# Spreading the state-space decay rows over the partitions: selector matmuls or broadcast reads from DRAM

## The chip, the cores and the metric

The kernel runs on one core of one Trainium2 chip. The metric is device time in microseconds (us) of one execution, smaller is better. The engines of the core are TensorE (PE in the profile; its weight loads are shown apart as PEld), VectorE (DVE), ScalarE (ACT), GpSimd (POOL) and SyncE (SP), which here only issues transfers. TensorE's clock has two levels, 1.2 and 2.4 GHz; the profile gives the granted clock as a share of the higher one.

## The reference, cut to what matters

Two layers, each a token-mixing sub-layer and an MLP, on 256 latent tokens and 256 context tokens of width 1024. The second layer doesn't need the context's output. One of the four mixers is a bidirectional state-space scan (SSD) in chunks of 128 tokens with 16 heads in 4 groups:

```
a_cum  = cumsum(dt * a)                       # over the 128 tokens of a chunk
seg    = a_cum[l] - a_cum[s]
decay  = exp(where(lower, seg, -inf))         # 128 x 128 for each chunk and head
y_diag = einsum(cb, decay, xdt)               # cb = C B^T of the group
y_off  = einsum(cm, states_in, exp(a_cum))
```

It runs once forward and once on the reversed sequence, and the two results are added. The other mixers (neighbourhood attention, pooling, Fourier), the gates, the output projection and the MLP are not touched by the change.

## The kernel before, in words

All arithmetic is float32. The large products (input projection, branch projections, MLP) split each 128-wide weight tile into a high part (ScalarE, L151) and a remainder (VectorE, L152) and run three passes on TensorE for each of 8 contraction tiles (`mm3`, L182): 24 matmuls of 512 columns in the first layer, of 512 or 256 in the second. Weight tiles `st` come through SP's queue (L145) into 3 buffers; their split pairs `whi`/`wlo` have 3 buffers too. The order of work is made by hand: `Driver` runs generators (`ssd_unit` for each of the 4 groups, two `attn_unit` after each), which yield so that one unit's projections fill TensorE while another's vector work runs. A planner then places the instructions on each engine's queue by priority; weight loads and splits get a priority 150 instructions earlier.

`dt_unit` computes the cumulative decays once for each layer. It transposes them to 64 rows (32 x direction + head) by 512 tokens in PSUM (`pr`, L486), and writes them as a high and a low part into R, and their exponentials into RE (L488 to L494).

In `ssd_unit`, a half-step `i` handles two heads `j`, each with two directions `d` (L594 to L617). For each (j, d), TensorE multiplies a column of the selector matrix, broadcast to 128 columns, with R: this spreads one row of the decays over all 128 partitions of a PSUM tile (L603). A second matmul adds the triangular mask (L604). ScalarE takes exp with the per-token bias `nAv`, one instruction for each chunk of 128 tokens (L607), into a tile `ex`. A third matmul spreads the row of RE (L610), and VectorE multiplies it with `Ct` into `e0` (L612). GpSimd adds the two directions (L614), VectorE multiplies by `cb` (L615), and after the next yield TensorE uses both products (L628, L631). A layer has 4 groups x 2 half-steps x 2 heads x 2 directions = 32 such (j, d). NT, the number of chunks, is 4 in the first layer and 2 in the second; NX is 512 and 256 tokens. The tiles `ex` and `e0` come from the pool `t2` (2 KB on each partition, 40 buffers), which most other 512-wide temporaries use too.

After the last group, `yt` (L663) is split (L196, L197) and goes into the SSD branch projection.

Of the kernel before, what the change touches and what calls it, by code (L numbers as in the profile page):

```python
# [9 lines left out]
F32 = mybir.dt.float32  # L10
F32R = mybir.dt.float32r
# [4 lines left out]
P = 128  # L16
# [42 lines left out]
def _const_layout():  # L59
    n = 0  # L60
    for name, w in (("ident", 128), ("triu", 128), ("tril", 128), ("cos", 256), ("sin", 256), ("sel2", 2),
                    ("maskf", 128), ("maskb", 128), ("sel", 32)):
        _CONST[name] = (n, w)
        n += w
    return n
# [8 lines left out]
def hybrid_backbone_kernel(ctx: ExitStack, tc: tile.TileContext, I, out, dbg=None):  # L74
# [10 lines left out]
    t2p = ctx.enter_context(tc.tile_pool(name="t2", bufs=40))  # L85
# [4 lines left out]
    drm = ctx.enter_context(tc.tile_pool(name="drm", bufs=1, space=bass.MemoryType.DRAM))  # L90

# [3 lines left out]
    def T2(shape, name, dt=F32):  # L95
        return t2p.tile(shape, dt, tag="t2", name=name)
# [10 lines left out]
    def PS(shape=(P, 512)):  # L107
        return pss.tile(list(shape), F32, tag="sm", name="psx")
# [5 lines left out]
    once = T2([P, NCONST - NKEEP], "once")  # L114
# [259 lines left out]
    def layer(l, need_ctx, h, ws, load_x, final, prepare=None):  # L374
# [51 lines left out]
        def dt_unit(ps):  # L426
# [55 lines left out]
            R = lay.tile([P, 4, P], F32R, tag="R", name="R", bufs=1)  # L482
# [4 lines left out]
            prv = pr[0:64, :].rearrange("p (t c) -> p t c", t=4)  # L487
            act.copy(R[0:64], prv)  # L488
            dve.tensor_tensor(R[64:128], prv, R.bitcast(F32)[0:64], op=ALU.subtract)
            RE = lay.tile([P, 4, P], F32R, tag="RE", name="RE", bufs=1)  # L490
            er = T2([64, 4, P], "er")
            act.activation(er, prv, AF.Exp)
            act.copy(RE[0:64], er)
            dve.tensor_tensor(RE[64:128], er, RE.bitcast(F32)[0:64], op=ALU.subtract)  # L494
            dtc.update(R=R, RE=RE, nA=v4(nA), coef=v4(coef), dec=v4(dec))

# [26 lines left out]
        def ssd_unit(g, ready=None):  # L523
# [16 lines left out]
            coefv, decv, nAv, R, RE = dtc["coef"], dtc["dec"], dtc["nA"], dtc["R"], dtc["RE"]  # L540
# [17 lines left out]
            for d in range(2):  # L558
                xw = T4([P, 4, 256], "xw")
                for t0, n in (((0, 1), (2, 2)) if d == 0 else ((1, 3),)):  # L560
                    dve.tensor_tensor(xw[:, t0:t0 + n].rearrange("p t (h c) -> p t h c", h=4),
                                      xk[:, t0:t0 + n].rearrange("p t (h c) -> p t h c", h=4),
                                      coefv[:, t0:t0 + n, d, 4 * g:4 * g + 4].unsqueeze(3).to_broadcast([P, n, 4, 64]),
                                      op=ALU.mult)
                xws.append(xw)
            yield "w", 1
# [27 lines left out]
            for i in range(2):  # L594
                M, CE = {}, {}
                for j in range(2):
                    hd = 4 * g + 2 * i + j
                    ed = []
                    for d in range(2):
                        c = 16 * d + hd  # L600
                        one = selr[:, c:c + 1].to_broadcast([P, P])
                        pv = PS().rearrange("p (t c) -> p t c", t=4)
                        pe.matmul(pv[:, 0:NT], one, R[:, 0:NT], start=True, stop=False)  # L603
                        pe.matmul(pv[:, 0:NT], identr, maskr[:, d:d + 1].to_broadcast([P, NT, P]), start=False, stop=True)  # L604
                        ex = T2([P, 4, P], "ex")
                        for t in range(NT):
                            act.activation(ex[:, t], pv[:, t], AF.Exp, bias=nAv[:, t, d, hd:hd + 1])  # L607
                        ed.append(ex)
                        pa = PS()
                        pe.matmul(pa.rearrange("p (t c) -> p t c", t=4)[:, 0:NT], one, RE[:, 0:NT], start=True, stop=True)  # L610
                        e0 = T2([P, 512], "e0")
                        dve.tensor_tensor(e0[:, 0:NX], Ct[:, 0:NX], pa[:, 0:NX], op=ALU.mult)  # L612
                        CE[j, d] = e0
                    pool.tensor_tensor(ed[0][:, 0:NT], ed[0][:, 0:NT], ed[1][:, 0:NT], op=ALU.add)  # L614
                    dve.tensor_tensor(ed[0][:, 0:NT], ed[0][:, 0:NT], cb[:, 0:NX].rearrange("p (t c) -> p t c", c=P),  # L615
                                      op=ALU.mult)
                    M[j] = ed[0]  # L617
                yield "w", 1
# [629 lines left out]
    sp.dma_start(once, I["consts"][:, NKEEP:NCONST])  # L1248
    identr = cst.tile([P, P], F32R, name="identr")
    act.copy(identr, ident)  # L1250
    maskr = cst.tile([P, 2, P], F32R, name="maskr")
    act.copy(maskr, once[:, 0:256].rearrange("p (d c) -> p d c", d=2))
    selr = cst.tile([P, 32], F32R, name="selr")
    act.copy(selr, once[:, 256:288])
# [30 lines left out]
def _constants():  # L1285
    c = np.zeros((P, NCONST), np.float32)

    def put(name, a):
        o, w = _CONST[name]
        c[:, o:o + w] = a  # L1290
# [12 lines left out]
    sel = np.zeros((P, 32))  # L1303
    for d in range(2):
        for h in range(16):
            sel[32 * d + h, 16 * d + h] = 1
            sel[64 + 32 * d + h, 16 * d + h] = 1
    put("sel", sel)
# [96 lines left out]
```

## Time and profile before

| | us |
|---|---|
| median of 3 runs | 2168.09 |
| lowest, highest | 2165.13, 2174.14 |
| the profiled execution | 2167.03 |
| its span, first to last instruction | 2164.9 |
| mean granted TensorE clock | 0.989 |

Busy times of an engine are unions over its instructions. A matmul's time runs from its start to its modelled end, and the next one starts before that; so the busy share of PE says that it had something in hand, and the distance from start to start says how fast it works. Where a row names a releaser, the time before it is idle time of that engine, and the releaser is what ended it. SPq rows are instructions of SP's queue; the time from there to landing is given apart.

### The profile page before, as it was taken

To read this page: it belongs to the slowest core of one execution; us is meant where nothing else is said; L and a number is where in the kernel's file an instruction comes from. 1 tells how busy PE (TensorE), PEld (TensorE's weight loads), DVE (VectorE), ACT (ScalarE), POOL (GpSimd) and SP (SyncE) were. 2 spreads that over 40 slices of the span, in tenths; PEclk is the share of its full clock that TensorE was granted. 3 is DMA by queue.
4 is the path that set the end of the run, shared out by engine and by line. 5 is a ranking of instruction groups with operands and counts; after the bars stand their busy time and mean duration, and the time that the engine had idled before them with its cause. 6 is when DMAs were issued, how large, how long until landed. Compare 5 with 4: busy or idle time off the path is not lost. (4 is left out here: it accounts for less than half of the span.)

```text
span 2164.9 us, 31409 instructions
## 1 busy us (share of the span) xinstructions
PE 2106.0 (97%) x12248; PEld 1740.0 (80%) x12248; DVE 1273.1 (59%) x2281; ACT 997.9 (46%) x1756; POOL 238.6 (11%) x244
## 2 busy tenths in 40 slices
PE   6999999999999999999999999999999999998998
PEld 3677777777888888878877887878787899987987
DVE  3686585854336544475333357687768557566557
ACT  3565565654323323334232233566656545445543
POOL 0001000010010010112011121001000000112111
PEclk8999999999999999999999999999999999999999
DMA  7523232332332531334343333423333466566554
GB/s 268 170 78 117 88 127 88 124 105 70 97 94 91 179 106 52 98 117 150 110 149 123 95 115 135 140 79 117 124 100 123 136 184 209 173 208 214 188 190 140
DMA packets 85379, 285.35 MB, mean 132 GB/s; under 512 B 9904, under 2 KB 13680, under 8 KB 85232
## 3 DMA queue, kind: packets, MB, share of 16 engines
q1 hardware_dynamic: 85232, 283.36, 40.9%
q8 instruction: 96, 1.57, 0.3%
q14 instruction: 51, 0.42, 0.1%
HBM read 281.19 MB, written 2.13 MB: 131 GB/s over the span
## 5 line engine op out<-in xcount | busy, mean ns | idle before, releaser
L152 DVE TENSOR_TENSOR wlo<-st,whi 128x1024 fp32r<-128x1024 f32 (+3 forms) x382 | 478.8, 1254 | 482.9 <-ACT whi L151 466.6
L151 ACT CAST whi<-st 128x1024 fp32r<-128x1024 f32 (+3 forms) x382 | 385.8, 1011 | 767.9 <-PE pm L182 539.6
L182 PE MATMUL pm<-h_hi,whi 128*128 128x512 f32 (+1 forms) x1944 | 680.4, 351 | 3.6 <-DVE qb L682 2.1
L182 PE MATMUL pm<-h_lo,whi 128*128 128x512 f32 (+1 forms) x1944 | 676.3, 348 | 3.1 <-DVE h_lo L364 3.0
L182 PE MATMUL pm<-h_hi,wlo 128*128 128x512 f32 (+1 forms) x1944 | 677.2, 349 | 0.3 <-DVE wlo L152 0.3
L182 PEld LDWEIGHTS pm<-h_hi,whi 128*128 128x128 f32 x1944 | 369.4, 190 | 56.5 <-issue 9.3
L182 PEld LDWEIGHTS pm<-h_lo,whi 128*128 128x128 f32 x1944 | 369.9, 190 | 47.2 <-DVE h_lo L364 3.9
L182 PEld LDWEIGHTS pm<-h_hi,wlo 128*128 128x128 f32 x1944 | 369.4, 190 | 47.0 <-issue 1.9
L191 PE MATMUL pm<-whi,part 128*128 128x512 f32 x784 | 243.4, 391 | 0.0
L182 PE MATMUL pm<-part,whi 128*128 128x512 f32 (+1 forms) x896 | 222.8, 338 | 2.9 <-DVE part L197 1.2
L182 PEld LDWEIGHTS pm<-part,whi 128*128 128x128 f32 x896 | 154.4, 190 | 23.1 <-DVE part L197 2.5
L191 PEld LDWEIGHTS pm<-whi,part 128*128 128x128 f32 x784 | 146.3, 188 | 30.6 <-issue 0.4
L191 PE MATMUL pm<-wlo,part 128*128 128x512 f32 x392 | 152.7, 390 | 0.0
L182 PE MATMUL pm<-part,wlo 128*128 128x512 f32 (+1 forms) x448 | 150.7, 336 | 0.5 <-DVE wlo L152 0.5
L1149 POOL TENSOR_TENSOR relu<-relu 128x512 f32<-128x512 f32 (+1 forms) x64 | 87.4, 1366 | 395.9 <-ACT relu L1146 370.8
L819 POOL TENSOR_TENSOR mg<-mg,gth 128x512 f32<-128x512 f32 (+1 forms) x48 | 53.3, 1111 | 533.1 <-DVE gth L818 466.4
L509 DVE SCALAR_TENSOR_TENSOR cacc<-cv,cols,cacc 128x512 f32<-128x512 f32 (+1 forms) x128 | 93.8, 733 | 8.9 <-ACT cacc L507 6.7
L182 PEld LDWEIGHTS pm<-part,wlo 128*128 128x128 f32 x448 | 85.1, 190 | 9.3 <-DVE wlo L152 0.7
L191 PEld LDWEIGHTS pm<-wlo,part 128*128 128x128 f32 x392 | 73.6, 188 | 15.7 <-DVE wlo L152 0.4
L283 PE MATMUL psx<-ad,csil 128*32 128x256 f32 x688 | 57.8, 405 | 9.3 <-DMA ad<-ada_w 8.9
L818 DVE SCALAR_TENSOR_TENSOR gth<-gth,pm 128x512 f32<-128x512 f32 (+1 forms) x48 | 26.6, 554 | 65.6 <-PE pm L182 65.6
L614 POOL TENSOR_TENSOR ex<-ex 128x512 f32<-128x512 f32 (+1 forms) x32 | 33.4, 1045 | 253.2 <-ACT ex L607 178.3
(270 smaller groups left out, 2594.3 us busy)
## 6 DMA issues: line engine op xcount, KB each, us to landing
st<-in_w SPq DMA_DIRECT2D x184, 512.0 KB, 3.6
ad<-ada_w SPq DMA_DIRECT2D x86, 512.0 KB, 3.6
st<-mlp_up_w SPq DMA_DIRECT2D x64, 512.0 KB, 3.5
st<-mlp_down_w SPq DMA_DIRECT2D x64, 512.0 KB, 3.6
bia<-rpb SPq DMA_DIRECT2D x16, 512.0 KB, 4.5
st<-ssd_out_w SPq DMA_DIRECT2D x16, 512.0 KB, 3.6
st<-na_out_w SPq DMA_DIRECT2D x16, 512.0 KB, 3.5
st<-mix_out_w SPq DMA_DIRECT2D x16, 512.0 KB, 3.7
```

Of the source, the lines that this page charges most:

```text
L151: act.copy(hi, st)
L152: dve.tensor_tensor(lo, st, hi.bitcast(F32), op=ALU.subtract)
L182: pe.matmul(ps, w(x, kw), rhs(a[y], ka), start=(i == 0 and j == 0), stop=(i == n - 1 and j == 2))
L191: pe.matmul(ps, a[y][k][:, P * t:P * t + P], w(x, i), start=(k == 0 and j == 0), stop=(k == KD - 1 and j == 2))
L283: pe.matmul(pa[32 * k:32 * k + 32, 0:256], csil[:, 4 * kc + k, :], st(k), start=(kc == 0), stop=(kc == 1), tile_position=(0, 32 * k))
L509: dve.scalar_tensor_tensor(acc, c[:, 0:ns, k:k + 256], col("convw", 5 * m + k), acc, op0=ALU.mult, op1=ALU.add)
L614: pool.tensor_tensor(ed[0][:, 0:NT], ed[0][:, 0:NT], ed[1][:, 0:NT], op=ALU.add)
L818: dve.scalar_tensor_tensor(th, th, 1.0, py[:, 0:NX], op0=ALU.add, op1=ALU.mult)
L819: pool.tensor_tensor(mg[m], mg[m], th, op=ALU.add)
L1149: pool.tensor_tensor(r2, r, r, op=ALU.mult)
```

## The change

The decay rows no longer go through TensorE. `dt_unit` copies the 64 x 512 cumulative decays (VectorE) and their exponentials (ScalarE) into two `t2` tiles and writes both to DRAM (`sums`, 128 KB each, SP's queue). `ssd_unit` reads each needed row back with a broadcast transfer that writes the same row to all 128 partitions: 8 transfers for each half-step (2 heads x 2 directions x {decays, exponentials}), on SP's queue, into `t2` tiles `line`. Those for half-step 0 are traced one yield earlier, those for half-step 1 behind half-step 0's vector work. VectorE adds bias and mask in place, one instruction for each chunk of 128 tokens; ScalarE takes one exp over the whole tile. The product with `Ct` reads the second line from SBUF in place of PSUM. R, RE, `identr`, `maskr` and `selr` go; `maskm` (1 KB on each partition) stays resident; `t2` gets 42 buffers.

```diff
-    t2p = ctx.enter_context(tc.tile_pool(name="t2", bufs=40))
+    t2p = ctx.enter_context(tc.tile_pool(name="t2", bufs=42))
+    sums = [[drm.tile([64, 512], F32, name=f"sums{l}{x}") for x in range(2)] for l in range(DEPTH)]
-    once = T2([P, NCONST - NKEEP], "once")
+    maskm = cst.tile([P, 2, P], F32, name="maskm")
...
-            R = lay.tile([P, 4, P], F32R, tag="R", name="R", bufs=1)
...
-            act.copy(R[0:64], prv)
-            dve.tensor_tensor(R[64:128], prv, R.bitcast(F32)[0:64], op=ALU.subtract)
-            RE = lay.tile([P, 4, P], F32R, tag="RE", name="RE", bufs=1)
-            er = T2([64, 4, P], "er")
-            act.activation(er, prv, AF.Exp)
-            act.copy(RE[0:64], er)
-            dve.tensor_tensor(RE[64:128], er, RE.bitcast(F32)[0:64], op=ALU.subtract)
+            for x in range(2):
+                rt = T2([64, 512], "rt")
+                if x:
+                    act.activation(rt, pr[0:64, :], AF.Exp)
+                else:
+                    dve.tensor_copy(rt, pr[0:64, :])
+                sp.dma_start(sums[l][x], rt)
...
+            def load_lines(i):
+                for j in range(2):
+                    for d in range(2):
+                        r = 32 * d + 4 * g + 2 * i + j
+                        for x in range(2):
+                            lines[j, d, x] = T2([P, 4, P], "line")
+                            sp.dma_start(lines[j, d, x].rearrange("p t c -> p (t c)")[:, 0:NX],
+                                         sums[l][x][r:r + 1, 0:NX].to_broadcast([P, NX]))
...
+            load_lines(0)
             yield "w", 1
...
-                        c = 16 * d + hd
-                        one = selr[:, c:c + 1].to_broadcast([P, P])
-                        pv = PS().rearrange("p (t c) -> p t c", t=4)
-                        pe.matmul(pv[:, 0:NT], one, R[:, 0:NT], start=True, stop=False)
-                        pe.matmul(pv[:, 0:NT], identr, maskr[:, d:d + 1].to_broadcast([P, NT, P]), start=False, stop=True)
-                        ex = T2([P, 4, P], "ex")
+                        ex, e0 = lines.pop((j, d, 0)), lines.pop((j, d, 1)).rearrange("p t c -> p (t c)")
                         for t in range(NT):
-                            act.activation(ex[:, t], pv[:, t], AF.Exp, bias=nAv[:, t, d, hd:hd + 1])
+                            dve.scalar_tensor_tensor(ex[:, t], ex[:, t], nAv[:, t, d, hd:hd + 1], maskm[:, d], op0=ALU.add,
+                                                     op1=ALU.add)
+                        act.activation(ex[:, 0:NT], ex[:, 0:NT], AF.Exp)
                         ed.append(ex)
-                        pa = PS()
-                        pe.matmul(pa.rearrange("p (t c) -> p t c", t=4)[:, 0:NT], one, RE[:, 0:NT], start=True, stop=True)
-                        e0 = T2([P, 512], "e0")
-                        dve.tensor_tensor(e0[:, 0:NX], Ct[:, 0:NX], pa[:, 0:NX], op=ALU.mult)
+                        dve.tensor_tensor(e0[:, 0:NX], Ct[:, 0:NX], e0[:, 0:NX], op=ALU.mult)
                         CE[j, d] = e0
...
+                if i == 0:
+                    load_lines(1)
                 yield "w", 1
```

## Rows read from the trace of the kernel before

**Rows 1.** The page, busy us, share of the span, instructions, by engine
```profile
PE 2106.0 (97%) x12248; PEld 1740.0 (80%) x12248; DVE 1273.1 (59%) x2281; ACT 997.9 (46%) x1756; POOL 238.6 (11%) x244
```
**Rows 2.** SSD stretches: us, PE, PEld, DVE, ACT, POOL busy; clock, DMA, GB/s
```profile
145.00:500.00 355.00, 353.73 (x2134) 276.35 (x2133) 237.56 (x531) 207.68 (x458) 31.53 (x28) 0.99 0.32 101
1440.00:1680.00 240.00, 239.77 (x1582) 195.91 (x1581) 178.66 (x424) 146.92 (x305) 20.51 (x25) 1.00 0.36 114
```
**Rows 3.** PE's waits, 95 to 520 us: us in total, times, longest
```profile
PE pm L182 <- DVE part L197: 0.8, 1, 0.8
```
**Rows 4.** The three selector lines, all of the span: duration min/median/max, first and last start
```profile
L603 PE MATMUL psx<-R,selr x64: 276/390/580, 151.3 to 1669.7; 128*128 128x512 f32 x32, 128*128 128x256 f32 x32
...
L604 PE MATMUL psx<-maskr,identr x64: 276/336/398, 151.5 to 1669.9; 128*128 128x512 f32 x32, 128*128 128x256 f32 x32
...
L610 PE MATMUL psx<-RE,selr x64: 274/388/501, 152.0 to 1670.0; 128*128 128x512 f32 x32, 128*128 128x256 f32 x32
```
**Rows 5.** Timeline, first layer: start us, duration us, engine, line, what
```profile
151.30 0.40 PE L603 MATMUL psx<-R,selr 128*128 128x512 f32 x1
151.30 0.19 PEld L604 LDWEIGHTS psx<-maskr,identr 128*128 128x128 f32 x1
151.53 0.39 PE L604 MATMUL psx<-maskr,identr 128*128 128x512 f32 x1
...
151.76 0.39 PE L182 MATMUL pm<-h_hi,whi 128*128 128x512 f32 x1
...
151.99 2.19 ACT L607 ACTIVATE ex<-psx,nA 128x128 f32<-128x128 f32 x8
...
155.84 0.40 PE L182 MATMUL pm<-h_hi,wlo 128*128 128x512 f32 x1
...
156.49 0.49 PE L610 MATMUL psx<-RE,selr 128*128 128x512 f32 x1 [0.24 <-DVE e L612]
```
**Rows 6.** Timeline, second layer, PE
```profile
1666.66 0.28 PE L604 MATMUL psx<-maskr,identr 128*128 128x256 f32 x1
1666.78 0.28 PE L610 MATMUL psx<-RE,selr 128*128 128x256 f32 x1
```
**Rows 7.** DVE by line and shape, all of the span: count, busy us, mean ns, idle before
```profile
L446 DVE SCALAR_TENSOR_TENSOR e<-e,s 128x128 f32<-128x128 f32 x12 | 3.4, 285 | 0.1
...
L917 DVE SCALAR_TENSOR_TENSOR f<-cs,fu,psx 128x129 f32<-128x129 f32 x18 | 5.7, 344 | 0.0
```
**Rows 8.** DVE by line and shape, 145 to 500 us
```profile
L612 DVE TENSOR_TENSOR e<-Ct,psx 128x512 f32<-128x512 f32 x32 | 21.5, 681 | 0.5
...
L615 DVE TENSOR_TENSOR ex<-ex,cb 128x512 f32<-128x512 f32 x16 | 11.1, 692 | 10.8 <-POOL ex L614 10.6
```
**Rows 9.** ACT by line and shape, all of the span
```profile
L646 ACT ACTIVATE sq<-ys 128x512 f32<-128x512 f32 x8 | 5.1, 632 | 7.0 <-DVE ys L645 7.0
```
**Rows 10.** ACT's waits, 145 to 500 us: us in total, times, longest
```profile
ACT whi L151 <- PE pm L182: 50.1, 17, 8.4
```
**Rows 11.** The page's DMA issues: count, KB each, median us to landing
```profile
gb<-gd SPq DMA_DIRECT2D x12, 256.0 KB, 4.7
...
gd<-grow SPq DMA_DIRECT2D x4, 8.0 KB, 3.2
```
**Rows 12.** SP's queue in time: start us, us, line, what
```profile
70.90 0.91 SPq L673 DMA_DIRECT2D bia<-rpb  x2
...
1936.25 8.93 SPq L268 DMA_DIRECT2D adh<-ada_w  x12
```
**Rows 13.** The stretch behind the 12 transfers of rows 12: columns as in rows 2
```profile
1940.00:1945.00 5.00, 5.00 (x26) 3.87 (x29) 3.50 (x6) 1.05 (x1) 0.00 (x0) 1.00 0.99 362
```
**Rows 14.** First use of the bias tiles, and the first layer's last `yt` and its split
```profile
L713 DVE CUSTOM_DVE_ANT_0 sc<-psx,bia x2: 421/423/425, 106.3 to 107.7; 128x256 f32<-128x256 f32 x2
...
L663 DVE SCALAR_TENSOR_TENSOR yt<-ys,cols,psx x2: 741/744/747, 487.7 to 488.4; 128x512 f32<-128x512 f32 x2
...
L196 ACT CAST part<-yt x8: 616/620/626, 505.2 to 509.8; 128x512 fp32r<-128x512 f32 x8
```

More of the change, by code (lines that the diff above doesn't have):

```diff
@@ L61, in _const_layout @@
     for name, w in (("ident", 128), ("triu", 128), ("tril", 128), ("cos", 256), ("sin", 256), ("sel2", 2),
-                    ("maskf", 128), ("maskb", 128), ("sel", 32)):
+                    ("maskf", 128), ("maskb", 128)):
         _CONST[name] = (n, w)
@@ L486, in dt_unit @@
                 pe.transpose(pr[0:64, P * t:P * t + P], av[:, t, :], ident)
-            prv = pr[0:64, :].rearrange("p (t c) -> p t c", t=4)
-            act.copy(R[0:64], prv)
-            dve.tensor_tensor(R[64:128], prv, R.bitcast(F32)[0:64], op=ALU.subtract)
-            RE = lay.tile([P, 4, P], F32R, tag="RE", name="RE", bufs=1)
-            er = T2([64, 4, P], "er")
-            act.activation(er, prv, AF.Exp)
-            act.copy(RE[0:64], er)
-            dve.tensor_tensor(RE[64:128], er, RE.bitcast(F32)[0:64], op=ALU.subtract)
-            dtc.update(R=R, RE=RE, nA=v4(nA), coef=v4(coef), dec=v4(dec))
+            for x in range(2):
[5 more added lines that the diff above has]
+                sp.dma_start(sums[l][x], rt)
+            dtc.update(nA=v4(nA), coef=v4(coef), dec=v4(dec))
         yt = {}
@@ L539, in ssd_unit @@
             yield "w", LAGS[0] + (LAGS[1] if ready else 0)
-            coefv, decv, nAv, R, RE = dtc["coef"], dtc["dec"], dtc["nA"], dtc["R"], dtc["RE"]
+            coefv, decv, nAv = dtc["coef"], dtc["dec"], dtc["nA"]
+            lines = {}
+            def load_lines(i):
[6 more added lines that the diff above has]
+                                         sums[l][x][r:r + 1, 0:NX].to_broadcast([P, NX]))
             xk = T4([P, 4, 256], "xk")
@@ L1247, in hybrid_backbone_kernel @@
     prepare(0)
[L1248 to L1254, printed above, removed]
+    sp.dma_start(maskm, I["consts"][:, NKEEP:NCONST].rearrange("p (d c) -> p d c", d=2))
     xt, h, ws = layer(0, True, h, first_weights(0, 1), load_in, False, prepare)
@@ L1302, in _constants @@
     put("sin", np.concatenate([-np.sin(ang), np.sin(ang)], 0))
[L1303 to L1308, printed above, removed]
     sel2 = np.zeros((P, 2))
```

## The prediction, made before the changed kernel was run

> **What bounds the kernel now.** First the page's busy shares: PE 97%, VectorE 59%, ScalarE 46% [rows 1]. These are means over stages, so I read the two stretches in which the changed lines run, 145 to 500 us and 1440 to 1680 us, by engine [rows 2]. The columns to look at are PE and DVE. PE has something in hand for 353.73 of 355 us and for 239.77 of 240; VectorE is busy for 237.56 (67%) and 178.66 (74%), ScalarE for 59% and 61%. DMA engines are busy a third of the time (101 and 114 GB/s).
>
> A busy PE need not be a PE at its pace, so next come its waits: in the first SSD stage the longest is 0.8 us [rows 3]. Then the pace: in the first layer a 512-column matmul starts 0.23 us behind the one before, though each is shown as 0.39 to 0.40 us long [rows 5]; in the second layer a 256-column one starts 0.12 us behind [rows 6]. Ordinary projection matmuls (L182) and selector matmuls stand in one stream at that same spacing. So in these stretches PE's queue is the bound, and an instruction taken from it is worth its spacing, not its shown duration, as long as the others keep up.
>
> A rule speaks against this. The Trainium skill (Trainium Kernel Development and Optimization, Performance Expectations) calls matmul busy time a bad measure and weight-load busy time a good one. Weight loads are busy for 276.35 of 355 us, 78% [rows 2]. But a load takes 0.19 us of a spacing of 0.23 [rows 5], so a full stream of this kind shows 83%. By that reading at most 1 - 78/83 = 6% of the stretch, 21 us, is unfilled; its price stands among the rivals as a mechanism of this kernel.
>
> **What is removed from PE.** 64 of each of the three selector matmuls, 32 of each with 512 columns and 32 with 256 [rows 4]. First layer: 96 x 0.23 = 22.1 us. Second: 96 x 0.115 = 11.1 us (two starts 0.12 apart, rounded [rows 6]; half the columns of 0.23). Together 33.2 us, all inside stretches that PE bounds. One more gain: a selector matmul at times waits for a PSUM buffer, as L610 at 156.49, which started 0.65 us behind the matmul before it instead of 0.23 [rows 5]. Such waits go; but PE's listed waits are small [rows 3], so I count nothing, and up to 10 us (24 such cases of 0.42) for the range.
>
> **What is added to VectorE.** 128 scalar-tensor-tensor instructions of 128 x 128 in the first layer, 64 in the second. The trace has none with a pointer scalar and two SBUF tensors at this size. Below: L446, 285 ns, constant scalar. Above: L917, 344 ns, pointer scalar and a PSUM operand [rows 7]. I take 0.32 us, nearer to L917 because of the pointer scalar: 41 us (36.5 to 44.0) and 20.5 us (18.2 to 22.0). The product with `Ct` costs the same from SBUF: L612 from PSUM took 681 ns, L615 from SBUF 692 [rows 8]. VectorE's load becomes 237.6 + 41 = 279 us in a stretch shortened to 333 us (84%), and 178.7 + 20.5 = 199 in 229 us (87%). It stays below PE, so the 61 us count at nothing; what covers them is the projection stream on PE. VectorE becomes the bound only if one of the new instructions took over 95/128 = 0.74 us.
>
> The Trainium skill (VectorE: DVE Perf Modes, The TRN2 errata) says that an SBUF operation pays a fixed latency for each instruction and advises tiles of at least 512 elements; four pieces of 128 go against that. The trace agrees: 285 to 344 ns for 128 columns [rows 7] against 692 for 512 [rows 8].
>
> **What moves on ScalarE.** Eight exps of 128 columns took 2.19 us, 0.27 each [rows 5]; one activation of 512 took 0.63 [rows 9]. A (j, d) goes from 1.09 to 0.63 us in the first layer. ScalarE isn't the bound: counted at nothing. The small work in `dt_unit` and at the start changes by a few instructions once a layer, in the shade of the projections: nothing.
>
> **What is added to SP's queue and the DMA engines.** 64 broadcast reads of 256 KB and 64 of 128 KB, and four writes of 128 KB. The nearest row is `gb`: the same form (one DRAM row to 128 partitions, 256 KB), landing 4.7 us after issue; `grow` to DRAM, the write ahead of it, takes 3.2 [rows 11]. A half-step's 8 reads are 2.1 MB in the first layer. Behind them on SP's queue stand weight loads. The price of such a burst is in the trace: 12 transfers of 256 KB were put on SP's queue from 1936.25 on [rows 12], the DMA engines were full (0.99, 362 GB/s), and PE was still busy for 5.00 of 5.00 us [rows 13]. By that rate a half-step's reads take 2.1 MB / 362 GB/s = 5.8 us (2.9 in the second layer). The weights have more than this in hand: three loaded tiles and three split pairs, each worth 24 x 0.23 = 5.5 us of PE in the first layer; ScalarE's weight casts wait for PE to free a pair (50.1 us in 17 waits [rows 10]). So the bursts count at nothing; without the cover they cost 8 x 5.8 + 8 x 2.9 = 70 us.
>
> **Where the new waits stand.** VectorE's first addition of a tile waits for its line; behind it on VectorE's queue are `wlo` splits, for which PE waits. ScalarE's exp now waits for VectorE instead of PE, with weight casts behind it. Lines can land early: a transfer goes out as soon as its buffer is free; the first two bias tiles went out at 70.90 us [rows 12] and were used at 106.3 [rows 14]. The decays are in DRAM long before the first half-step at 151 us. Each half-step's chain grows, by 16 additions x 0.32 less 4 exps x (1.09 - 0.63) = 5.1 - 1.8 = 3.3 us in the first layer and, with half of both, 1.6 us in the second. What comes late next is `yt` of the last group: ready at 488 us, split from 505.2 us [rows 14], 17 us in hand. I add 1 us for new waits of PE, about the longest one now.
>
> **The sum.** 2167.0 (profiled execution) - 33.2 + 1 = 2134.8 us. The median of the runs lies 1.1 us above the profiled one: 2136 us, 1.5% faster.
>
> **The rivals.**
> (1) *VectorE's queue takes PE's place, or PE had room.* VectorE is in order and near 85%; additions, attention's row operations and `wlo` splits bunch around half-steps. With each half-step's longer chain fully exposed: 8 x 3.3 + 8 x 1.6 = 39 us, 2136 + 39 = 2175. With half exposed: 2155. The 21 us of unfilled PE worked out above would give 2157, the same place. For it: VectorE's share of 84 to 87%. Against it: the planner fills PE with projections, which need only their weights, and splits have priority.
> (2) *Slower: the lines hold SP's queue.* The reads need `t2` buffers, 8 more at a time beside those of the half-step before, and the pool has only 2 more. If a line's issue waits for a buffer, every weight load behind it waits too, and reads then land only when needed. Price: the 70 us above uncovered, 2136 + 70 = 2206. It decides when queue hold and transfer together pass the weights' cover, some 5.5 us x 3 loaded tiles = 16 us. Against it: rows 13, where PE ran on through a burst half as long again.
> (3) *It doesn't do what it says:* lines land late, the half-steps wait on them as they waited for PE before, and what PE gains it idles: 33 us back, 2168.
>
> **How the numbers follow.** A difference under 0.5% (10.8 us: 2157 to 2179) is about what a measurement of this kernel can't tell from no change. Forecast 0.55; its own range is 2122 (PSUM waits gone, and some) to 2148 (a third of the chain exposed). Rival 1 at its half 0.15, at its full size 0.09; rival 3 0.08; rival 2 0.13. Faster: 0.55 + 0.15 = 0.70. Same: 0.09 + 0.08 = 0.17. Slower: 0.13. The range 2122 to 2172 leaves out rival 2 and the top of rival 1, less than 2 in 10.
>
> **What the profile after should show.** No L603, L604, L610; about 192 matmuls fewer. Both SSD stretches shorter by some 22 and 11 us, with PE still busy over 98%. VectorE up by some 60 us in all, the new instructions near 0.32 us; exps fewer by 128, near 0.63 us. 128 more transfers, landing in 4 to 8 us, out well before use. VectorE's waits on them would show rival 3, waits of PE on `wlo` rival 1, weight casts waiting for `st` transfers rival 2. I am wrong if VectorE's additions cost far above 0.34 us, or if a broadcast read is much slower when 8 go at once.

## The result, and the profile after

The changed kernel takes 2182.92 us (2180.32 to 2186.18), 1.0068 times the time before, with a 95% interval of 1.0049 to 1.0087: 0.7% slower. I had forecast 2136 and a range that ended at 2172.

The page of the kernel after, busy us by engine [rows 1]:

```profile
PE 2100.3 (96%) x12056; PEld 1716.7 (79%) x12056; DVE 1316.8 (60%) x2471; ACT 973.7 (45%) x1621; POOL 248.5 (11%) x244
```

The 192 selector matmuls are gone (12248 to 12056), yet PE is busy for only 6 us less, and the span has grown by 16 us. To see where, I divide the span at points that every kernel of this study has: the start of the first cumulative-sum matmul of each layer (L469 before), of the first split of `yt` (L196), and of the first mixing split after the branches (L1002 before). All starts come from the traces of the profiled executions; the stages are their differences, so a column adds up to a span and not to a median.

| stage, us | before | after | e1 | e2 | e9 | e13 |
|---|---|---|---|---|---|---|
| up to layer 1's SSD | 95.3 | 95.9 | 98.9 | 100.1 | 95.8 | 95.7 |
| SSD stage, first layer | 409.9 | 421.4 | 419.6 | 410.3 | 401.7 | 399.8 |
| branches, first layer | 408.1 | 413.5 | 408.1 | 413.5 | 407.4 | 408.3 |
| mixing and MLP, to the next SSD | 493.3 | 495.9 | 494.8 | 496.9 | 492.2 | 492.1 |
| SSD stage, second layer | 298.0 | 294.9 | 294.1 | 299.0 | 292.2 | 283.9 |
| branches, second layer | 222.0 | 221.0 | 223.1 | 221.3 | 223.8 | 221.8 |
| rest of the span | 238.3 | 238.6 | 240.5 | 238.5 | 238.9 | 239.8 |

(e1 to e13 are the experiments below. The first stage differs by up to 5 us between kernels that do the same in it, so I read nothing from it.) Two things stand out in the column after. The first SSD stage, which should have lost 22 us, gained 11.5. And the branches, where no line was changed, gained 5.4.

The first SSD stage by engine, before and after (columns as in rows 2):

```profile
95.25:505.20 409.95, 407.54 (x2467) 316.62 (x2468) 277.92 (x635) 244.43 (x536) 33.44 (x30) 0.99 0.32 104
```
```profile
95.85:517.20 421.35, 398.98 (x2371) 305.76 (x2372) 307.51 (x762) 226.98 (x438) 36.92 (x30) 0.97 0.48 142
```

PE's idle time grew from 2.4 to 22.4 us, and the granted clock fell from 0.99 to 0.97. Summed over windows of 10 us, the time lost to a granted clock below 1 is 3.4 us before and 11.9 after. PE's waits in this stretch after the change (columns as in rows 3) say what it waited for:

```profile
PE psx L284 <- DMA ad<-ada_w: 16.4, 4, 5.4
PE psx L636 <- DVE line L621: 1.5, 2, 0.8
PE pm L183 <- ACT zz L650: 1.4, 1, 1.4
```

Three waits of about 5 us (5.06, 4.87 and 5.41; the fourth is 1.06) are for tiles of `ada_w`, the weights of the modulation, which the prediction never mentioned. They come through SP's queue into 2 buffers (L273), and their small matmuls stand in PE's queue between the projections. SP's queue after the change, around one of the three:

```profile
199.78 6.76 SPq L549 DMA_DIRECT2D line<-sums  x8
206.59 1.79 SPq L681 DMA_DIRECT2D bia<-rpb  x1
208.48 7.67 SPq L549 DMA_DIRECT2D line<-sums  x8
216.50 2.34 SPq L273 DMA_DIRECT2D ad<-ada_w  x2
```

Sixteen broadcast reads, 4.2 MB, go out nearly back to back, and the two `ad` loads stand behind them for 16.7 us. PE at the same time:

```profile
220.94 0.39 PE L183 MATMUL pm<-h_hi,wlo 128*128 128x512 f32 x1
226.38 1.08 PE L284 MATMUL psx<-ad,csil 128*32 128x256 f32 x8 [5.06 <-DMA ad<-ada_w]
...
229.59 0.63 PE L711 MATMUL psx<-kk,qa 128*128 128x512 f32 x1
230.02 0.63 PE L712 MATMUL psx<-kk,qb 128*128 128x512 f32 x1
```

After 5 us without work PE runs on at a spacing of 0.43 us for 512 columns instead of 0.23. The windows around it (columns as in rows 2) show the granted clock:

```profile
215.00:225.00 10.00, 6.33 (x28) 4.81 (x26) 7.66 (x17) 4.85 (x8) 1.29 (x1) 1.00 0.97 286
225.00:235.00 10.00, 8.62 (x66) 6.92 (x67) 5.10 (x22) 3.01 (x9) 0.00 (x0) 0.66 0.31 108
```

0.66 is the mean of a stretch in which the clock stood partly on its lower level, 1.2 GHz. So a 5 us wait costs more than 5 us. In the first window the DMA engines are full (0.97) but move 286 GB/s, not the 362 of rows 13.

The new instructions themselves are about as expected (all of the span; count, min/median/max ns; then the page's transfers with their median us to landing):

```profile
L614 DVE SCALAR_TENSOR_TENSOR line<-line,nA,maskm x192: 326/344/829, 144.2 to 1690.3; 128x128 f32<-128x128 f32 x192
...
L616 ACT ACTIVATE line<-line x64: 399/542/647, 145.4 to 1690.6; 128x512 f32<-128x512 f32 x32, 128x256 f32<-128x256 f32 x32
```
```profile
line<-sums SPq DMA_DIRECT2D x64, 256.0 KB, 7.7
...
line<-sums SPq DMA_DIRECT2D x64, 128.0 KB, 5.7
```

### The profile page after: what moved, and what is told of

It is laid out like the page before. It is cut to its first block, busy times and chain, and to the rows that moved or that the text cites. A ratio compares the mean times of both kernels' runs of the same rounds, so it can differ in the third digit from the quotient of the medians.

```text
span 2181.1 us, 31269 instructions
## 1 busy us (share of the span) xinstructions
PE 2100.3 (96%) x12056; PEld 1716.7 (79%) x12056; DVE 1316.8 (60%) x2471; ACT 973.7 (45%) x1621; POOL 248.5 (11%) x244
## 5 line engine op out<-in xcount | busy, mean ns | idle before, releaser
L192 PEld LDWEIGHTS pm<-whi,part 128*128 128x128 f32 x784 | 146.3, 188 | 30.9 <-issue 0.4
L620 POOL TENSOR_TENSOR line<-line 128x512 f32<-128x512 f32 (+1 forms) x32 | 41.2, 1289 | 291.3 <-ACT line L616 206.6
```

The costliest lines, as they stand in the source:

```text
L192: pe.matmul(ps, a[y][k][:, P * t:P * t + P], w(x, i), start=(k == 0 and j == 0), stop=(k == KD - 1 and j == 2))
```

## The experiments

Four theories were open. L (placement): the edit moved the weight tiles in SBUF, and that alone costs PE. Q (queue): the bursts of reads hold up what stands behind them. B (the reads themselves): 128 reads of one DRAM row are slower than other reads, which makes Q's bursts long. V (VectorE): its additions are not hidden.

### Placement: e1 and e2

In the compiled programs the first `whi` buffer begins at byte 76928 of each partition before and at 72192 after, and the other buffers of `whi` and `wlo` follow at steps of 4096; `h`, the activations that these weights multiply, begins at 1152 in both. Modulo 256 that is 128 for all before; after, the weights have 0 and `h` 128. e1 is the changed kernel with 128 spare bytes ahead of the weights, e2 the kernel before with the same spare bytes. The order of instructions on every engine stays as it was.

```diff
+    pad = cst.tile([P, 32], F32, name="pad")
+    pool.memset(pad, 0.0)
     cv = []
```

> The changed kernel with one unused 128-byte tile among the constants, so that every SBUF tile behind it lies 128 bytes further; the order of the instructions on all engines stays the same. Theory L (place of the weight tiles): the projection matmuls (L183, operands h and whi/wlo, 5832 of them) had 17 us more busy time after the change with the same count, because the weight tiles came to lie 128 bytes away, modulo 256, from where they lay against h. Then this kernel is 13 to 17 us faster than the changed one: 2166 to 2170 us, and 512-column L183 matmuls start 0.227 us apart again. Rival Q (all of the loss is SP's queue and ada_w transfers that come late): no change, 2183 us.

Measured: 2178.34 us, 4.6 less than after; 1.0048 (1.0031 to 1.0065) of before.

> The kernel before with the same unused 128-byte tile; the order of the instructions stays the same. Theory L: the weight tiles leave their place against h, 13 to 17 us slower: 2181 to 2185 us. Rival Q: no change, 2168 us.

Measured: 2182.65 us, 1.0070 (1.0051 to 1.0090) of before. Moving the tiles by 128 bytes costs 0.7% with nothing else changed. One line of the first layer's branches in before, after, e1 and e2, in this order (count, busy us, mean ns):

```profile
L182 PE MATMUL pm<-h_hi,whi 128*128 128x512 f32 x325 | 127.0, 391 | 0.0
```
```profile
L183 PE MATMUL pm<-h_hi,whi 128*128 128x512 f32 x328 | 130.0, 396 | 0.0
```
```profile
L185 PE MATMUL pm<-h_hi,whi 128*128 128x512 f32 x333 | 130.1, 391 | 0.0
```
```profile
L184 PE MATMUL pm<-h_hi,whi 128*128 128x512 f32 x328 | 130.0, 396 | 0.0
```

391 where `h` and the weights have the same place modulo 256, 396 where they differ, and the branches take 408.1 us in before and e1, 413.5 in after and e2. It is the distance between the two operands that goes with the time, not the place of the weights alone: where both operands had moved by the same amount (`part` lies at 128 modulo 256 before and at 0 after, like `whi`), the pages of before and after have the same 391 ns:

```profile
L191 PE MATMUL pm<-whi,part 128*128 128x512 f32 x784 | 243.4, 391 | 0.0
```
```profile
L192 PE MATMUL pm<-whi,part 128*128 128x512 f32 x784 | 243.6, 391 | 0.0
```

So L is a cause and explains the branches to the digit. It isn't the main one: e1 still pays in the first SSD stage (419.6 us), with 17.4 us of waits for `ad`. I had expected 2166 to 2170 of it if L were all. All later kernels keep the weights at 128 modulo 256.

### The queue: e3, e8, and the pair e4 and e5

e3 is e1 with the lines issued from ScalarE's queue instead of SP's.

```diff
-                            sp.dma_start(lines[j, d, x].rearrange("p t c -> p (t c)")[:, 0:NX],
+                            act.dma_start(lines[j, d, x].rearrange("p t c -> p (t c)")[:, 0:NX],
```

> The changed kernel with the 128-byte shift, and the 128 broadcast reads issued from ScalarE's queue instead of SP's. Theory Q (16 reads in a row hold SP's queue, and the ada_w transfer behind them comes 5 us late for its matmul, with PE idle and then at the lower clock): the three stalls of the first layer go, some 20 us of idle time and 8 of clock: 2135 to 2150 us. Rival B (the DMA engines are full, whichever queue): the ada_w transfers still land late behind the reads, PE still idles on them: within 8 us of the shifted kernel, 2160 to 2175. Rival A (ScalarE held by issuing and by waits for a free buffer): slower than the shifted kernel.

Measured: 2186.58 us, 1.0085 (1.0069 to 1.0102). The waits did not go, they moved. VectorE's and PE's waits of e3 in the first SSD stage:

```profile
DVE line L616 <- DMA line<-sums: 20.9, 12, 6.4
```
```profile
PE psx L286 <- DVE s L599: 4.7, 2, 2.5
...
PE psx L286 <- DMA ad<-ada_w: 1.2, 1, 1.2
```

Now `ad` is in time and the lines are late, and VectorE's in-order queue hands that on to PE. ScalarE is held too, by issuing:

```profile
208.87 7.97 ACTq L551 DMA_DIRECT2D line<-sums  x5
...
216.88 0.37 ACT L596 COPY s<-psx 128x256 f32<-128x256 f32 x1 [7.54 <-DMA line<-sums]
```

Five reads occupy its queue for 7.97 us, and the copy behind them comes after 7.54 us of idle time. Of the three forecasts rival A's came out, 8.2 us slower than e1. The first SSD stage is no longer than in e1 (419.4 and 419.6 us; PE idle 19.7 and 24.2); the loss lies in the second layer's, 302.7 us against 294.1. The Trainium skill (DMA: Bandwidth & Descriptors, Rules for kernel authors) says that spreading transfers over issuing engines gains no bandwidth, only time of issue. This run agrees as far as the time goes, and the time of issue came back on ScalarE; the rate of the reads was not compared.

e8 is e1 with `ada_w`'s loads put 150 instructions earlier in the planner's order, as weight loads are.

```diff
-        sp.dma_start(st, src)
+        with tc.high_priority(offset=AHEAD):
+            sp.dma_start(st, src)
```

> The changed kernel with the 128-byte shift; the ada_w loads get the same priority as the weight loads (150 instructions earlier), so they may go ahead of the broadcast reads on SP's queue. Theory Q: no PE wait on ada_w transfers in the first layer's SSD stage, 12 to 25 us faster than the shifted kernel: 2153 to 2166 us. Rival V: the waits move to other releasers, within 5 us of 2178.

Measured: 2165.74 us, 0.9978 (0.9966 to 0.9989); 12.6 us less than e1. PE's wait for `ad` in the stage is 1.1 us. That is the upper end of theory Q's range: PE is still idle for 18.0 us in the stage (24.2 in e1), now on short results of VectorE and ScalarE, and the time lost to a lower clock is 5.1 us (11.9).

e4 is e1 with the `ada` steps taken out of the first SSD stage altogether, into the branches' loop; e5 does the same to the kernel before, as a control.

```diff
-FILL = ((1,1,2,8,4),(0,1,1,10,0))
+FILL = ((0,0,0,8,4),(0,0,0,10,0))
...
+                if b == 1:
+                    ada(l, (4, 2)[l])
```

> The changed kernel with the 128-byte shift; the modulation products (ada_w loads and their matmuls) that the attention units carry in both layers are moved into the second branch's loop, so that no ada_w transfer stands behind the broadcast reads. Theory Q: no PE stall on ada_w in either SSD stage; 20 to 30 us faster than the shifted kernel, less what the moved products cost in their new place: 2138 to 2152 us; against the kernel before with the same move 25 to 33 us faster. Rival V (VectorE's longer half-steps hold PE): PE idles in the SSD stages just as much, on other releasers; gain under 10 us against the kernel before with the same move.

> The kernel before, unshifted, with the same move of the modulation products out of the attention units into the second branch's loop: the control for the changed kernel with the move (2181.5 us). Theory Q (late ada_w transfers are what costs the changed kernel its gain): this control is slower than the kernel before by what the moved products cost in their new place, 2195 to 2210 us, so that the change, with ada out of the way, gains 15 to 30 us. Rival V (VectorE's half-steps hold PE whatever stands behind the reads): the control takes 2168 to 2185 us, the change gains under 10 us.

Measured: e4 2181.53 us, e5 2186.09. (The move itself costs 16 us: it shortens the SSD stage of the kernel before by 20.1 us and lengthens its branches by 30.9. Only the difference between the two kernels counts here.) With no `ada_w` tile to be late in the SSD stages, the change gains 4.6 us by the medians, not 33, and the intervals overlap; e5 lies just above rival V's range and below theory Q's. The first SSD stage without `ada` work, e4 and then e5:

```profile
97.71:483.80 386.09, 367.44 (x2081) 288.12 (x2080) 306.79 (x730) 220.98 (x419) 39.95 (x30) 0.99 0.38 112
```
```profile
96.99:486.80 389.81, 380.66 (x2177) 305.41 (x2176) 273.03 (x603) 238.02 (x517) 36.48 (x30) 0.99 0.22 68
```

PE's busy time falls by 13 us, its idle time rises from 9.2 to 18.7, at the same clock. The largest wait behind it is no transfer:

```profile
PE psx L638 <- DVE line L623: 4.4, 5, 1.1
```

With 2.6 us on the product with `Ct` that is 7.0 of the 9.5 us by which the idle time grew. Late reads are not behind it: VectorE waits for lines for 1.7 us in this stage. So late `ada_w` tiles are not all; VectorE holds PE too.

### VectorE: e6 and e10

e6 is the kernel before, in which the row still comes by selector matmul, but the mask matmul is gone and VectorE adds bias and mask, straight from PSUM; no line is read from DRAM.

```diff
-                        pe.matmul(pv[:, 0:NT], identr, maskr[:, d:d + 1].to_broadcast([P, NT, P]), start=False, stop=True)
...
-                            act.activation(ex[:, t], pv[:, t], AF.Exp, bias=nAv[:, t, d, hd:hd + 1])
+                            dve.scalar_tensor_tensor(ex[:, t], pv[:, t], nAv[:, t, d, hd:hd + 1], maskm[:, d], op0=ALU.add,
+                                                     op1=ALU.add)
+                        act.activation(ex[:, 0:NT], ex[:, 0:NT], AF.Exp)
```

> The kernel before with the VectorE part of the change alone: selector matmuls for both rows stay, the mask matmul (L604) goes, VectorE adds bias and mask out of PSUM in 128-column pieces, ScalarE takes one exp over the tile; no broadcast read. Weight tiles lie as in the kernel before. Removed from PE: 32 x 0.23 + 32 x 0.115 = 11 us. Theory Q: VectorE's additions are hidden, 2157 to 2166 us. Rival V: the longer half-steps hold PSUM buffers and PE's products, 2175 us or more.

Measured: 2179.07 us, 1.0047 (1.0030 to 1.0065). PE lost 64 matmuls, worth 32 x 0.23 + 32 x 0.115 = 11 us by the spacing, and the kernel got 9 us slower: VectorE's part costs about 20 us by itself. The instructions are not dearer than thought (median 347 ns), so it is likely their place: they stand in the chain of a half-step and ahead of other work on VectorE's in-order queue. One thing is not separated from this: in e6 they read PSUM and hold its buffers, which the additions of the changed kernel don't.

e10 is e1 without the additions; the exponential is taken of the row as read.

> The changed kernel with the 128 spare bytes, without VectorE's addition of decay and mask (the 192 small instructions, 61 us); the exponential is taken of the row as it was read. Theory V (the additions lengthen the half-steps and so hold PE, besides the bursts): 2162 to 2172, that is 6 to 16 us under the 2178.3 of the kernel with them. Rival D (only the reads cost; VectorE's additions are hidden as I predicted): 2175 to 2181, with PE's wait on ad unchanged at 15 to 19 us.

Measured: 2167.51 us, 0.9997 (0.9982 to 1.0012), 10.8 us less than e1, with 12.9 us of waits for `ad` left in the stage (17.4 in e1, so part of the gain comes by way of them). In theory V's range again.

### The reads: e7, e9 and e11

e7 is e1 with each read taking 128 different rows of constants instead of one row 128 times: the same number, size and place of transfers, the decays left out.

```diff
-                                         sums[l][x][r:r + 1, 0:NX].to_broadcast([P, NX]))
+                                         sums[l][x][:, 0:NX])
```

> The changed kernel with the 128-byte shift; each read takes 128 different DRAM rows (constants) in place of one row 128 times, the same bytes, the same number of transfers: the decays and their exponentials in DRAM are left out, so the output isn't the reference's. Theory B1 (reading one row 128 times is what makes the bursts slow: 265 to 290 GB/s at full DMA share against 362 to 395 with plain rows): reads land in about 6 us instead of 7.7, the ada_w stalls shrink by a third or more, 2160 to 2172 us. Rival B2 (the bytes and their order count, not the source): same as the shifted kernel, 2178 us.

Measured: 2156.39 us, 0.9931 (0.9911 to 0.9950): 22 us less than e1, more than any theory had asked. The wait for `ad` in the stage falls to 1.6 us, the clock loss from 11.9 to 3.4 us. (The trace is of its fastest execution, 2148.33 us; the other three took 2155.9 to 2157.1.) That gain is to be had with the decays kept, if a row has several copies. e9 writes each row eight times and lets partition p read copy p mod 8:

```diff
-    sums = [[drm.tile([64, 512], F32, name=f"sums{l}{x}") for x in range(2)] for l in range(DEPTH)]
+    sums = [[drm.tile([64, 8, 512], F32, name=f"sums{l}{x}") for x in range(2)] for l in range(DEPTH)]
-                sp.dma_start(sums[l][x], rt)
+                sp.dma_start(sums[l][x], rt.unsqueeze(1).to_broadcast([64, 8, 512]))
-                                         sums[l][x][r:r + 1, 0:NX].to_broadcast([P, NX]))
+                                         sums[l][x][r:r + 1, :, 0:NX].to_broadcast([16, 8, NX]))
```

> The changed kernel with the 128 spare bytes, and the rows kept eight times in DRAM: each of the two writes per layer stores every row as eight neighbouring copies of 2 KB (1 MB a write instead of 128 KB), and each of the 128 line reads takes copy p mod 8 for partition p. Bytes read, number of reads, and all engine work stay as they are. Theory B (128 reads of one and the same DRAM row are slow, so the burst holds the queue and ada_w's tiles come late): close to the kernel that read 128 different rows (2156.4), a little above for the larger writes: 2154 to 2165, PE's wait on ad in the first SSD stage under 6 us, line reads at 5.7 to 6.5 us to landing. Rival N (that kernel gained because it left out the decays, or because its reads had no small source written shortly before): 2173 to 2183, wait on ad 15 us or more.

Measured: 2154.94 us, 0.9933 (0.9911 to 0.9955): 23.4 us less than e1 and faster than the kernel before. The wait for `ad` is halved, to 8.4 us, not under 6 as I had said; the longest is 2.8 us, and the clock loss is back at 3.4 us. Windows of 2 us within the same burst, four of after, two of e9 and two of e7 (columns as in rows 2; the last two are the DMA engines' share and GB/s):

```profile
204.00:206.00 2.00, 2.00 (x10) 1.40 (x8) 1.32 (x5) 0.69 (x2) 0.00 (x0) 1.00 0.34 135
...
208.00:210.00 2.00, 1.92 (x9) 1.06 (x7) 1.97 (x6) 1.47 (x4) 0.70 (x1) 1.00 1.07 259
210.00:212.00 2.00, 1.73 (x8) 1.17 (x7) 2.00 (x6) 0.59 (x3) 0.57 (x1) 1.00 1.03 226
...
216.00:218.00 2.00, 2.00 (x10) 1.61 (x10) 2.00 (x5) 1.04 (x2) 0.00 (x0) 1.00 1.01 355
```
```profile
205.00:207.00 2.00, 2.00 (x22) 1.13 (x15) 1.72 (x8) 1.32 (x3) 0.00 (x0) 1.00 1.05 276
207.00:209.00 2.00, 2.00 (x11) 1.57 (x10) 2.00 (x4) 1.83 (x5) 1.30 (x1) 1.00 1.09 282
```
```profile
205.00:207.00 2.00, 2.00 (x13) 1.55 (x10) 2.00 (x7) 1.69 (x4) 0.51 (x1) 1.00 1.04 411
207.00:209.00 2.00, 2.00 (x10) 1.70 (x9) 2.00 (x5) 0.79 (x3) 0.78 (x1) 1.00 1.03 392
```

At 208 to 212 us, with the DMA engines full, reads of one row move some 240 GB/s, where eight copies give 280 and 128 rows 400. The one-row burst isn't slow throughout, it is uneven: 355 GB/s in one window, and engines that are two thirds idle in another. Its 2048 packets of 2 KB say the same. With one row (after) the median packet takes 84 ns and the mean is 127; 11% take over 200 ns, the longest 939. With eight copies (e9) the median is 120 and the mean 118, with 128 rows (e7) 84 and 87, and under 1% take over 200 in either. So eight copies are not fast, they are even. Landing follows: 7.7 us after (8.0 in e1), 6.7 in e9 (I had said 5.7 to 6.5), 5.9 in e7. From a burst's first read to the `ad` loads behind it pass 18.1, 16.4 and 17.5 us in e1 and 14.3, 14.4 and 13.8 in e9, and PE then waits 1.5 us for the tile that was 5.1 late. So B is shown: the repetition of one row is what makes the bursts long enough to hurt. Why single packets of such a read take so long, no run tells. The cost is steep: of the 27.1 us between the two profiled executions, 17.9 lie in the first SSD stage (PE idle 13.4 us in place of 24.2, clock loss 3.4 in place of 11.9), for some 3 us of queue time in each of three bursts.

e11 has the copies and `ada_w` first.

> Eight copies of each row and ada_w's loads put ahead of the lines in SP's queue. If late ada_w tiles are the only way in which the bursts cost time, either remedy alone takes all of it, and both together give no more than the better one: 2154 to 2165. If the slow reads also cost PE through VectorE's wait for lines and the other loads behind them, both give more: 2142 to 2154.

Measured: 2156.32 us, 0.9944 (0.9927 to 0.9961). Both remedies together give no more than the copies, so they act on the same loss.

### Closing the sum: e13, and the versions e12, e14 and e15

e13 has the copies and leaves the additions out (the edits of e9 and e10 together).

> Eight copies of each row, and VectorE's additions of decay and mask left out, so that both suspected costs are gone at once and what is left of the change is the removed matmuls, the moved exponentials and the reads. Theory C (slow single-row reads and VectorE's additions are the two costs; placement is undone by the 128 spare bytes): near my forecast of 2136, 2134 to 2146, that is 9 to 20 us under the kernel with eight copies (2154.9). Rival: the additions only cost where the bursts have already upset the order: 2150 to 2157, and another 15 us of the change would stay without a cause.

Measured: 2145.91 us, 0.9892 (0.9876 to 0.9909), 9.0 us less than e9, at the edge of what theory C expected. Of the 10.6 us between the two profiled executions 8.3 lie in the second layer's SSD stage and 1.9 in the first's; between e1 and e10, with the bursts as they were, it was 1.4 and 8.1 of 12.8. So where the additions cost their time seems to depend on what else is late.

e12 keeps the arithmetic, but adds the mask in one instruction per tile and gives the bias back to ScalarE (on top of e11).

```diff
-                        for t in range(NT):
-                            dve.scalar_tensor_tensor(ex[:, t], ex[:, t], nAv[:, t, d, hd:hd + 1], maskm[:, d], op0=ALU.add,
-                                                     op1=ALU.add)
-                        act.activation(ex[:, 0:NT], ex[:, 0:NT], AF.Exp)
+                        dve.tensor_tensor(ex[:, 0:NT], ex[:, 0:NT], maskm[:, d:d + 1].to_broadcast([P, NT, P]), op=ALU.add)
+                        for t in range(NT):
+                            act.activation(ex[:, t], ex[:, t], AF.Exp, bias=nAv[:, t, d, hd:hd + 1])
```

> As the run with copies and ada_w first, but VectorE adds the mask in one instruction per tile (512 or 256 columns) and the decay goes back to ScalarE as the exponential's bias, four or two exponentials of 128 columns per tile as before the change. VectorE's additions fall from 192 instructions to 64. Theory V: 3 to 10 us under the run with copies and ada_w first. If VectorE's additions are hidden: within 2 us of it, or above, since ScalarE gets the small exponentials back.

Measured: 2151.24 us, 0.9913 (0.9883 to 0.9943), 5.1 us less than e11, though the intervals overlap. The new sum takes a mean of 685 ns for a tile of 512 columns and 435 for 256, where four or two pieces had a median of 344 each.

e14 is e9 with three buffers for `ada_w` (`wad` 3, `t2` 40).

> Eight copies of each row and three buffers for ada_w's tiles instead of two (the pool of 2 KB tiles goes back from 42 to 40 for the space). PE waited 8.4 us for ada_w's tiles in the first SSD stage with eight copies. If that wait still costs what it shows: 2146 to 2152. If what waits behind VectorE's longer half-steps takes its place, as it did when ada_w was put first: 2153 to 2158.

Measured: 2151.10 us, 0.9915 (0.9900 to 0.9931). PE's wait for `ad` is no longer among its leading waits in the stage; the medians differ by 3.8 us from e9, the intervals overlap: a gain not shown. e15 puts copies, the third buffer and the single mask addition together.

> Eight copies of each row, three buffers for ada_w's tiles, and the mask added once per tile with the decay back in the exponential's bias (the three edits that each gained or seemed to gain by themselves). If the gains add up: 2145 to 2149. If each only takes the place of another wait: 2150 to 2154, no better than with two of them.

Measured: 2144.84 us, 0.9902 (0.9885 to 0.9918), beside 2165.84 for the kernel before: 1.0% faster than before, and 1.7% than after by the medians. Against e14 (0.9915) the intervals overlap, so whether the gains add up isn't told. Its first SSD stage takes 400.1 us, as e14's does (400.3).

## Why the prediction was wrong, step by step

From the forecast of 2136 to the 2182.9 measured are 46.9 us. By medians: placement 4.6 (after to e1), the repeated row 23.4 (e1 to e9), VectorE's additions 9.0 (e9 to e13), and 9.9 left (e13 to 2136). The shares depend on the order in which they are taken: the intervals of e1 and after overlap, and the same 128 bytes cost 14 us in the kernel before (e2).

- *What bounds the kernel, and the price of the matmuls taken from PE:* the price was right. Between before and e13, PE's busy time in the first SSD stage falls from 407.5 to 387.0 us, 20.5 against the 22.1 of the sum. As time it came out in the second layer, whose stage shrinks by 14.1 against 11.1; the first layer's shrinks by 10.1, and most of the rest is idle time of PE. So in the second layer PE had no room to spare; whether it had in the first, as the 21 us among the rivals would have it, no run tells.
- *"So the bursts count at nothing":* the step that failed worst. The cover that I named was for projection weights, three tiles and three split pairs, and they did hold: no wait for `st` or `wlo` is among PE's leading ones after. But SP's queue carries other things. I never listed what else stands behind the reads, and so missed `ada_w`, with two buffers, whose matmuls stand in PE's in-order queue. Three further errors sat in the same term. I reckoned one half-step's 8 reads, 2.1 MB; two sets went out together, 4.2 MB. I took 362 GB/s from plain rows [rows 13]; reads of one row gave 226 to 259 at 208 to 212 us, and the whole burst was uneven. And `gb`'s 4.7 us [rows 11] was the price of the same form, but not of 16 of them in a row; four more of that form, on the same line of the kernel before, had landed after 7.5 us, and I left them out (the DMA issues of before):

```profile
gb<-downb SPq DMA_DIRECT2D x4, 256.0 KB, 7.5
```

- *The price of an idle PE* was not in the sum: with each 5 us wait came a granted clock of 0.66 to 0.81 over the 10 us around or after it, 8.5 us over the stage (11.9 less 3.4).
- *Rival 2 (lines hold SP's queue)* named this mechanism, at 0.13, but with projection weights as its victim and a limit of 16 us from their cover. Rows 13, which I held against it, showed plain rows, and 5 us of them. The trace of before goes on: five weight loads later in the same queue come two loads of `ad`, PE waits for them 2.84 and 1.92 us, and in 1960 to 1970 us it is busy for 3.97 us at a granted clock of 0.61. The first of the two waits:

```profile
1957.96 1.91 SPq L272 DMA_DIRECT2D ad<-ada_w  x2
```
```profile
1962.32 1.08 PE L283 MATMUL psx<-ad,csil 128*32 128x256 f32 x8 [2.84 <-DMA ad<-ada_w]
```

The page of before has these waits too, 8.9 us in all, the largest entry among PE's waits there, so the stream with the least cover could be read before the change:

```profile
L283 PE MATMUL psx<-ad,csil 128*32 128x256 f32 x688 | 57.8, 405 | 9.3 <-DMA ad<-ada_w 8.9
```

- *VectorE's additions "count at nothing":* wrong, though the size of each was right (344 ns, at the upper bound given). e6 prices them at about 20 us with the reads absent, e10 at 10.8, e13 at 9.0. I had worked out the longer chain of a half-step (3.3 and 1.6 us) and then called it hidden because VectorE's share stays below PE's. A share over a stage says nothing about a chain inside it. Rival 1 had the mechanism and, at half its size, 2155, which is where e9 lands (2154.9). The agreement is partly luck, since additions account for 9 of these 19 us.
- *Rival 3* fell in its own terms: VectorE waits 8.3 us in all for lines after the change (6.3 at the additions, 2.0 at the products with `Ct`).
- *Placement* was in no step. Nothing in the profile of before tells it; only a comparison of the addresses does.
- *What stays open:* 9.9 us. PE's idle time in the first SSD stage is 12.8 us in e13 and 13.6 in e14, 2.4 before. In e13 3.6 us of it are still for `ad`; the rest, and all of it in e14, are waits of at most 2.5 us, nearly all on short results of VectorE and ScalarE (`adat`, `adarows`, `s`, `line`). That the removed matmuls had stood in these gaps is likely, and is only argued: no run separates it from the writes of `sums`, from the order of the queues, or from GpSimd's sums of the two directions, whose mean for 512 columns is 1292 ns before, 1573 after and 1604 in e13.

## What to carry to other kernels

Before a burst of transfers is counted as hidden, list everything that stands behind it in its queue, with its own number of buffers and the place of its consumer in an in-order engine: the stream with the least cover decides, not the largest one, and the waits that its engine already has in the trace of before point to it. A broadcast read from DRAM should have several copies of its row to read from, and its price is that of the burst, not of a single transfer. When an unrelated stage gets slower after a change of tiles, compare the addresses of the two matmul operands before looking for a cause in the code.

## What the runs showed of the hardware that was not expected

- Reads that take one DRAM row for all 128 partitions move 135 to 355 GB/s in the windows of 2 us shown of one burst (226 to 259 at 208 to 212 us); with the DMA engines full, eight copies move 276 to 297, 128 different rows 388 to 411. Two thirds of the one-row packets are as short as those of 128 rows (under 90 ns), and the loss is in the long ones. The Trainium skill (HBM Reference, Specifications) gives about 425 GB/s for a core that streams alone; the 128 rows come near it, the one row does not.
- A shift of the weight tiles by 128 bytes against the moving tile makes a 512-column matmul of this kind 396 ns long instead of 391. The spacing in a run of them rises from 0.2265 us (20 steps from 212.72 to 217.25 before) to 0.2324 (21 from 216.06 to 220.94 after). Matmuls of 256 columns show nothing of it: 285 to 286 ns before, 285 to 287 after. Over the kernel it cost 14 us (e2). That the place modulo 256 is what counts fits all four kernels; other distances weren't tried.
